# A hybrid decoder layer on one core: x's transposes become side threads, TensorE gets matmuls to run before x arrives, and the planner's account of DMA landings gets other numbers

## The chip, the core and the metric

The kernel runs on one core of a Trainium2 chip. A core has a matrix engine (TensorE, PE in the profile), a vector engine (VectorE, DVE), an activation engine (ScalarE, ACT), a general engine (GpSimd, POOL) and a sync engine (SyncE, SP), which here only issues DMAs. The engines run side by side; each works through its own list of instructions strictly in order and waits for the others on semaphores. The metric is the device time of one execution in microseconds, of which three runs are given.

## The reference, cut to what matters

One decoder layer is computed for 256 tokens of width 2048 in float32:

```
h    = rmsnorm(x, norm_mix_w)                      # x: 256 x 2048
proj = h @ w_in        # q, k, v, z, b, a, p_in, g_a, g_b  (2048 x 14368)
q,k,v = silu(causal_dwconv(q,k,v)); q,k l2-normalised per head of 128
o    = gated_delta_rule(q, k, v, g, beta)          # 16 heads, chunks of 64 in the reference
y_a  = rmsnorm(o) * silu(z)
y_b  = causal_multiscale_pool(p_in) @ pool_w * pool_scale
x   += (sigmoid(g_a) * y_a + sigmoid(g_b) * y_b) @ w_out
h    = rmsnorm(x, norm_ffn_w);  gate, up = split(h @ w_up)      # w_up: 2048 x 11264
x   += (gelu(causal_dwconv(gate) + b) * up) @ w_down            # w_down: 5632 x 2048
return rmsnorm(x, norm_final_w)
```

## The kernel before, in words

**Chunks.** Every large weight matrix is read from HBM in chunks of 256 rows by 512 columns (512 KB). `fetch` issues the DMA of a chunk into one of four `raw` buffers, `cast` rounds it on ACT to `whi`, `split` forms the rest `wlo = raw - whi` on DVE, and `gemm_a` multiplies: 12 matmuls of 128 x 512 a chunk, that is for two rows of 128 of the chunk and two blocks of 128 tokens each `xhi*whi`, `xlo*whi`, `xhi*wlo`. There are 530 chunks. In this text they are counted from 0 in the order of use: 0 to 7 are the keys of head group 0, 8 and 9 (of another shape, 8 matmuls each) feed beta and the decays, 10 to 17 are queries, 18 to 25 values; 26 to 49 are keys, queries and values of head group 1, 50 to 57 the gate z of group 0, and so on. There are four of each of `whi` and `wlo`, so the cast of a chunk cannot start before PE is done with the chunk four places earlier, and the DMA of a chunk not before the split of the chunk four places earlier.

**Order of the work.** The program is written in the order of PE's matmuls. Between them `side()` puts in other work: first the pipeline of chunks (split, cast, fetch, each when its inputs are thought to be there), then a step of one of the threads: Python generators that are started with `spawn(gen, rank)` and yield at each change of engine. A class `Plan` keeps a clock for each engine and decides when a step's turn has come. The engines execute what stands in their lists, whenever its inputs come; only the order is fixed by the plan. Its account of DMAs (`Plan.dma`, line 50) adds bytes divided by 240e3 per us to a queue, and 2 us until the landing.

**Around the change, at the start.** SP issues x in four parts of 512 columns, each followed by the DMA of a weight chunk. `x_turned(k2)` (line 411) transposes columns 256 k2 to 256 k2 + 255 of x on PE (4 transposes into a PSUM tile, `psb` for even k2, `psa` for odd), then ACT writes the rounded half `xhi` with the norm's weight as a scale (2 instructions), and DVE the rest `xlo` (2 instructions). These eight turns are called in the program's main line: turn 0 before the first GEMM, turn c + 1 from `x_next(c)`, ahead of chunk c. Threads that start there are `norms` (8 squares of x on ACT with their sums), `vectors` (small vectors, read by DMAs on ACT's queue and transposed on PE) and `matrices`.

**Around the change, later.** The work of a head group runs in threads beside the GEMMs of the next. Of it the prediction speaks of: `flip` (a DVE transpose `tn`, then 4 DMAs of 128 KB to DRAM), `decays` (`dec<-rund`, a DMA of 512 KB to all partitions, two selects on POOL, then 24 exponentials on ACT in two halves of 12, for which ACT's table may have to be loaded), and in `gdn` the solve: `cdd`, four DMAs `lb`, then 31 pairs of DVE operations `tmp` and `tb`, which get shorter from 128 x 248 on. Who holds `dec` gives it back when the last `ga` of the group before has been formed on DVE.

Of the kernel before, what the change touches and what calls it, by code (L numbers as in the profile page):

```python
# [13 lines left out]
P = 128  # L14
# [17 lines left out]
class Plan:  # L32
# [4 lines left out]
    def __init__(self):  # L37
        self.t = dict(PE=0.0, V=0.0, A=0.0, G=0.0, S=0.0)
        self.ready = self.base = 0.0
        self.queue = 0.0  # L40
        self.table = "s"

    def at(self, time):
# [6 lines left out]
    def dma(self, eng, out):  # L50
        n = 4
        for d in out.shape:
            n *= d
        self.t[eng] = max(self.t[eng], self.base) + (0.42 if eng == "S" else 0.1)
        self.queue = max(self.queue, self.t[eng]) + n / 240e3
        self.ready = max(self.ready, self.queue + 2.0)

    def op(self, eng, name, out, args, kw):
# [49 lines left out]
def kernel(  # L108
# [20 lines left out]
    plan = Plan()  # L129
# [14 lines left out]
    def nm(s):  # L144
        cnt[0] += 1
        return f"{s}_{cnt[0]}"

    def pa(shape=(P, 512)):
        return psg.tile(list(shape), F32, tag="a", name=nm("psa"))
# [7 lines left out]
    def bank():  # L157
        while len(banks) > 1 and not (banks[-2] and banks[-2] <= now["PE"]):
            yield
        banks.append(None)  # L160
        return len(banks) - 1

    def leave(n):
        banks[n] = plan.ready
# [6 lines left out]
    def take(*tags):  # L171
        while taken_by(tags):
            yield
        held.update((tag, 1e9) for tag in tags)
# [19 lines left out]
    def follow(th, step):  # L194
        if isinstance(step, tuple):
            step, th[0] = step
        th[3] = step or th[3]
        threads.sort(key=lambda th: th[:2])

    def spawn(gen, rank=1):  # L200
        cnt[0] += 1
        threads.append([rank, cnt[0], gen, None, plan.ready])
        follow(threads[-1], next(gen))
# [32 lines left out]
    def until(done):  # L236
        while not done():
            if not side():
                now["PE"] += 0.25
# [138 lines left out]
    ones = cpool.tile([P, P], F32, name="ones")  # L378
# [4 lines left out]
    epsx = cpool.tile([P, 2], F32, name="epsx")  # L383
# [11 lines left out]
    x0 = []  # L395
    for c in range(4):
# [3 lines left out]
        x0.append((xc, plan.ready))  # L400
        fetch()

    plan.at(nmready)
    nmw = cpool.tile([P, KD], F32, name="nmw")
    pv = pb()
    nc.tensor.transpose(pv[:, :KD], nmrows, ident[:KD, :KD])
    nc.vector.tensor_copy(nmw, pv[:, :KD])
    xhl = big.tile([P, KD, 2, S], F32R, tag="xhl", name="xhl")
    xhi, xlo = xhl[:, :, 0, :], xhl[:, :, 1, :]

    def x_turned(k2):
        pt = (pa if k2 % 2 else pb)([P, 2, S])
        plan.at(x0[k2 // 2][1])
        for kk in range(2):
            k = 2 * k2 + kk
            for t in range(2):
                nc.tensor.transpose(pt[:, kk, t * P : (t + 1) * P], x0[k // 4][0][:, t, (k % 4) * P : (k % 4 + 1) * P],
                                    ident)
        for kk in range(2):
            k = 2 * k2 + kk  # L420
            nc.scalar.activation(xhi[:, k, :], pt[:, kk, :], AF.Copy, scale=nmw[:, k : k + 1])
        for kk in range(2):
            k = 2 * k2 + kk
            nc.vector.scalar_tensor_tensor(xlo[:, k, :], pt[:, kk, :], nmw[:, k : k + 1], xhi[:, k, :].bitcast(F32),
                                           op0=ALU.mult, op1=ALU.subtract)

    def xh(k, t):
        return xhi[:, k, t * P : (t + 1) * P]
# [573 lines left out]
    for g in range(4):  # L1002
        vts = []
        res = []
        turns.append(res)
        done = []

        def keys(e, g=g, done=done):
            d = yield from flip(mp, e, "ev", g)
            yield from take("k", "q")  # L1010
            kq = mp.tile([P, 4, 2, S], F32, tag="kq", bufs=1, name=nm("kq"))
            done.append(kq)
            yield from conv_silu(d, 1, g, kq[:, :, 0, :])
            done.append(plan.ready)

        def queries(e, g=g, done=done):
            d = yield from flip(mp, e, "ev", g)
            while not done:
                yield
            yield from conv_silu(d, 0, g, done[0][:, :, 1, :])  # L1020
            done.append(plan.ready)

        def heads(g=g, vts=vts, res=res, done=done):
            yield "S"
            yield from take("dec0", "dec1")
            dec0 = mp.tile([P, 4, S], F32, tag="dec0", name=nm("dec0"))
            dec1 = mp.tile([P, 4, P], F32, tag="dec1", name=nm("dec1"))
            yield from decays(g, dec0, dec1)
            while len(done) < 3:
                yield  # L1030
            plan.at(max(plan.ready, *done[1:]))
            yield "PE"
            yield from take("heads")
            yield from gdn(g, done[0], vts, dec0, dec1, res)

        def values(e, g=g, vts=vts):
            d = yield from flip(mp, e, "ev", g)
            yield from take("vT")
            vT = mp.tile([P, 4, S], F32, tag="vT", bufs=1, name=nm("vT"))
            yield from conv_silu(d, 2, g, vT)  # L1040
            yield "V"
            yield from take("vt")
            vt = mp.tile([P, 2, 4, P], F32, tag="vt", name=nm("vt"))
            yield from flip_back(mp, vT, vt, "vT")
            vts.append(vt)
            vts.append(plan.ready)

        if g == 0:
            x_turned(0)

            def x_next(c):
                if c == 1:
                    plan.at(x0[0][1])
                    spawn(norms(), -1)
                if c == 2:
                    spawn(vectors(), 0)
                    spawn(matrices(), 1)
                if c < 7:
                    x_turned(c + 1)

            ps = gemm_a(xh, xl, KD, before=x_next)
            pba = pm()[:, 0, :].rearrange("p (a s) -> p a s", a=2)
            for c in range(2):
                hi, lo = weights()
                for kk in range(8):
                    k = 8 * c + kk
                    mm(pba, hi[:, kk, :], xhl[:, k], start=(k == 0), stop=(k == KD - 1))
                side()

            def start(pba=pba, heads=heads):  # L1070
                yield from strengths(pba)
                yield from heads()
        else:
            ps = gemm_a(xh, xl, KD)
        spawn(keys(evict(ps)), g)
        if g == 0:
            spawn(start(), -1)
        spawn(queries(evict(gemm_a(xh, xl, KD))), g)
        if g:
            spawn(heads(), g)  # L1080
        spawn(values(evict(gemm_a(xh, xl, KD))), g)
        if g:
            gates(g - 1)
# [215 lines left out]
```

## Time and profile before

| what | value |
|---|---|
| three runs | 1565.99, 1567.35, 1568.28 us; median 1567.35 us |
| the profiled execution | 1567.87 us, its span 1566.1 us |
| PE busy | 1540.2 us (98%), 7212 matmuls |
| DVE, ACT, POOL busy | 1036.6 us (66%), 787.2 us (50%), 68.0 us (4%) |
| HBM read / written | 309.11 MB / 23.10 MB, 212 GB/s over the span |
| granted clock of PE, mean | 0.994 |

In a row of a timeline stand the start in us from the span's start, the duration of the whole row, the engine, the source line, the operation, written tile <- read tiles, shapes and the number of instructions merged into the row; in brackets the engine's idle time ahead of it and what ended it. Nearly all rows name line 94, the wrapper that counts the plan's time. An engine's name with a q (SPq, ACTq) is the sequencer that issues DMAs. A row of waits gives the sum in us, the number of waits and the longest. A row of windows gives for a stretch the length, busy time of each engine with its number of instructions, the granted clock of PE (1.00 is full speed), the DMA engines' share and GB/s. PE's matmuls overlap, so that the spacing of their starts tells the pace and not the duration of one.

### The profile page before, as it was taken

Reading aid. Unit: us, or ns where it says so; the run is one execution under the profiler, and the core shown is the slowest. Engines: PE = TensorE matmul, PEld = TensorE weight load, DVE = VectorE, ACT = ScalarE, POOL = GpSimd, SP = SyncE. Lnnn points to the kernel's source line nnn. Section 1 sums busy time; section 2 is a strip of 40 time slices with the busy share of each in tenths; the row PEclk is TensorE's granted clock in tenths of the full one; section 3 lists DMA queues with packets and bytes.
Section 4 is the critical chain, followed back from the end, with each engine's and each line's share of the span. In section 5 each row is a group of like instructions: output and inputs, shape, how many; then the busy total and the mean of one; then the engine's idle time right before and its main releaser. Section 6 shows DMA issues by size and latency. Waiting matters only on the chain.

```text
span 1566.1 us, 19803 instructions
## 1 busy us (share of the span) xinstructions
PE 1540.2 (98%) x7212; PEld 1261.8 (81%) x7212; DVE 1036.6 (66%) x1488; ACT 787.2 (50%) x1036; POOL 68.0 (4%) x109
## 2 busy tenths in 40 slices
PE   7999999999999999999999999999999999999996
PEld 5787788787878887888888888888888888888885
DVE  4778967788778766865565666666667666544444
ACT  6474574456545854454454445454454444433334
POOL 1201000100010001000000000000000000000000
PEclk9999999999999999999999999999999999999998
DMA  7887974788568857774756888888888887665663
GB/s 227 218 257 191 264 205 140 182 253 245 147 188 234 239 162 202 191 205 133 252 179 187 246 230 233 247 248 250 243 231 232 255 244 210 233 197 191 220 195 110
DMA packets 342585, 333.52 MB, mean 213 GB/s; under 512 B 181031, under 2 KB 201559, under 8 KB 342359
## 3 DMA queue, kind: packets, MB, share of 16 engines
q1 hardware_dynamic: 339776, 327.78, 72.0%
q10 hardware_dynamic: 2710, 4.48, 0.8%
q8 instruction: 56, 0.92, 0.2%
q14 instruction: 43, 0.34, 0.1%
HBM read 309.11 MB, written 23.10 MB: 212 GB/s over the span
## 4 chain that ended last, share of the span: by engine, by line
PE 92%; DVE 3%; DMA 2%; ACT 1%; SPq 1%; issue 1%; DVEq 0%; ACTq 0%
PE psm L94 79%; PE psa L94 8%; PE psb L94 5%; DMA raw<-in_w_in_dram 2%; DVE wlo L94 1%; DVE tmp L94 1%; SPq L94 1%; DVE tb L94 1%; ACT whi L94 0%; DVE xt L94 0%; DVE tn L94 0%; DMA x<-in_x_dram 0%; ACT sqj L94 0%; DVE cy L94 0%; ACT ev L94 0%
## 5 line engine op out<-in xcount | busy, mean ns | idle before, releaser
L94 DVE TENSOR_TENSOR wlo<-raw,whi 128x1024 fp32r<-128x1024 f32 x528 | 641.4, 1222 | 409.7 <-ACT whi L94 404.2
L94 ACT CAST whi<-raw 128x1024 fp32r<-128x1024 f32 x530 | 555.7, 1052 | 621.9 <-PE psm L94 452.2
L94 PE MATMUL psm<-whi,xhl 128*128 128x512 f32 x1792 | 566.8, 398 | 4.3 <-ACT whi L94 4.0
L94 PE MATMUL psm<-whi,fhl 128*128 128x512 f32 x1408 | 433.6, 389 | 0.0
L94 PEld LDWEIGHTS psm<-whi,xhl 128*128 128x128 f32 x1792 | 334.7, 190 | 75.3 <-ACT whi L94 5.1
L94 PE MATMUL psm<-wlo,xhl 128*128 128x512 f32 x896 | 352.7, 394 | 4.2 <-DVE wlo L94 4.2
L94 PEld LDWEIGHTS psm<-whi,fhl 128*128 128x128 f32 x1408 | 264.1, 188 | 54.9
L94 PE MATMUL psm<-wlo,fhl 128*128 128x512 f32 x704 | 273.9, 389 | 0.0
L94 PEld LDWEIGHTS psm<-wlo,xhl 128*128 128x128 f32 x896 | 169.6, 189 | 43.3 <-DVE wlo L94 7.0
L94 PEld LDWEIGHTS psm<-wlo,fhl 128*128 128x128 f32 x704 | 132.1, 188 | 27.4
L94 PE MATMUL psm<-whi,hhi 128*128 128x512 f32 x176 | 68.5, 389 | 0.0
L94 PE MATMUL psm<-whi,hlo 128*128 128x512 f32 x176 | 68.5, 389 | 0.0
L94 PE MATMUL psm<-wlo,hhi 128*128 128x512 f32 x176 | 68.5, 389 | 0.0
L94 ACT ACTIVATE fev<-psm,rs 128x512 f32<-128x512 f32 x44 | 27.9, 686 | 46.2 <-PE psm L94 46.2
L94 PE MATMUL psm<-whi,mhi 128*128 128x512 f32 x128 | 50.5, 394 | 0.0
L94 PE MATMUL psm<-wlo,mhi 128*128 128x512 f32 x128 | 50.0, 390 | 0.0
L94 PE MATMUL psm<-whi,mlo 128*128 128x512 f32 x128 | 49.9, 390 | 0.0
L94 DVE SCALAR_TENSOR_TENSOR cy<-kq,cqw,cy 128x255 f32<-128x255 f32 (+2 forms) x96 | 44.1, 479 | 1.6
L94 DVE SCALAR_TENSOR_TENSOR y<-gs,cfw,y 128x255 f32<-128x255 f32 x88 | 42.6, 484 | 3.1
L94 DVE TENSOR_TENSOR tmp<-lb,tb 128x248 f32<-128x248 f32 (+30 forms) x124 | 37.1, 299 | 4.7 <-DMA lb<-cdd 1.8
L94 DVE TENSOR_TENSOR tb<-tb,tmp 128x248 f32<-128x248 f32 (+30 forms) x124 | 37.3, 301 | 4.3
L94 DVE STREAM_TRANSPOSE tn<-fev 128x1024 f32<-128x1024 f32 x22 | 27.3, 1242 | 17.1 <-ACT fev L94 15.2
(194 smaller groups left out, 1238.2 us busy)
## 6 DMA issues: line engine op xcount, KB each, us to landing
raw<-in_w_in_dram SPq DMA_DIRECT2D x226, 512.0 KB, 4.6
raw<-in_w_up_dram SPq DMA_DIRECT2D x176, 512.0 KB, 4.9
raw<-in_w_down_dram SPq DMA_DIRECT2D x88, 512.0 KB, 4.5
flip<-tn SPq DMA_DIRECT2D x136, 128.0 KB, 3.3
raw<-in_w_out_dram SPq DMA_DIRECT2D x32, 512.0 KB, 4.3
gs<-flip SPq DMA_DIRECT2D x11, 512.0 KB, 5.9
us<-flip SPq DMA_DIRECT2D x11, 512.0 KB, 6.6
kq<-flip SPq DMA_DIRECT2D x8, 512.0 KB, 6.4
```

Of the source, the lines that this page charges most:

```text
L94: r = getattr(self.eng, op)(out, *args, **kw)
```

## The change

1. `Plan`: the queue's account starts at 2.5 us instead of 0, and a DMA takes bytes / 170e3 us where the rows of its tile are at most 32 elements long, bytes / 380e3 otherwise, instead of bytes / 240e3 for all.
2. Before the DMA of the norm's weights is waited for, ACT copies a column of `epsx` to itself (which makes it load its table there), and PE runs 6 matmuls of 128 x 128 on a tile of ones; after the transpose of the norm's weights 3 more.
3. `x_turned` becomes a thread with a yield at each change of engine, and takes a PSUM bank of the plan; a turn starts once the turn four before it is done by the plan. All eight are spawned at once with rank -3 (the lowest rank goes first), and the GEMM's chunk c only waits in the plan until turn c is done.

```diff
     def __init__(self):
-        self.queue = 0.0
+        self.queue = 2.5
...
-        self.queue = max(self.queue, self.t[eng]) + n / 240e3
+        self.queue = max(self.queue, self.t[eng]) + n / (170e3 if out.shape[-1] <= 32 else 380e3)
...
+    def run_up(n):
+        warm = pa()
+        for _ in range(n):
+            tc.nc.tensor.matmul(warm[:, 0:P], ones, ones, start=True, stop=True)
+
+    tc.nc.scalar.copy(epsx[:, 0:1], epsx[:, 0:1])
+    run_up(6)
     plan.at(nmready)
...
     nc.vector.tensor_copy(nmw, pv[:, :KD])
+    run_up(3)
...
+    turned = []
 
     def x_turned(k2):
+        yield "PE"
+        while len(turned) < k2 - 3:
+            yield
+        n = yield from bank()
         pt = (pa if k2 % 2 else pb)([P, 2, S])
-        plan.at(x0[k2 // 2][1])
...
+        yield "A"
...
+        yield "V"
...
+        leave(n)
+        turned.append(plan.ready)
...
-            x_turned(0)
+            for k2 in range(8):
+                plan.at(x0[k2 // 2][1])
+                spawn(x_turned(k2), -3)
 
             def x_next(c):
+                until(lambda: len(turned) > c)
...
-                if c < 7:
-                    x_turned(c + 1)
```

No matmul of the GEMMs and no DMA is added or taken away. Since the plan's times are others, the lists of all engines are in another order in many places up to the end of the attention part. Three of these places are shown.

**ACT, from the kernel's start.** `xhl<-psb` and `xhl<-psa` are the scaled copies of a turn (even and odd k2), `CAST whi` the casts of chunks 0, 1, 2. Before:

```order
L94 ACT_TABLE_LOAD
L94 ACTIVATE xhl<-psb_122,nmw 128x256 x2
L94 ACTIVATE xhl<-psa_132,nmw 128x256 x2
L94 CAST whi_141<-raw_87 128x1024
L94 ACTIVATE xhl<-psb_160,nmw 128x256 x2
L94 CAST whi_169<-raw_91 128x1024
L94 CAST whi_179<-raw_95 128x1024
```

Now:

```order
L408 ACT_TABLE_LOAD
L408 COPY epsx<-epsx 128x1
L94 ACTIVATE xhl<-psb_135,nmw 128x256 x2
L94 CAST whi_142<-raw_87 128x1024
L94 ACTIVATE xhl<-psa_144,nmw 128x256 x2
L94 CAST whi_161<-raw_91 128x1024
L94 ACTIVATE xhl<-psb_169,nmw 128x256 x2
L94 CAST whi_183<-raw_95 128x1024
```

The casts of chunks 0 and 1 each stand one turn earlier: chunk 0's ahead of turn 1, chunk 1's ahead of turn 2.

**DVE, a little later.** `wlo` are the splits of chunks, `xhl` with `xhl` among its inputs the `xlo` of a turn. Before, from the split of chunk 3 on:

```order
L94 TENSOR_TENSOR wlo_222<-raw_99,whi_208 128x1024
L94 TENSOR_TENSOR wlo_236<-raw_151,whi_234 128x1024
L94 SCALAR_TENSOR_TENSOR xhl<-psb_244,nmw,xhl 128x256 x2
L94 TENSOR_TENSOR wlo_255<-raw_183,whi_253 128x1024
L94 SCALAR_TENSOR_TENSOR xhl<-psa_285,nmw,xhl 128x256 x2
```

Now, from the same split on:

```order
L94 TENSOR_TENSOR wlo_241<-raw_99,whi_208 128x1024
L94 TENSOR_TENSOR wlo_243<-raw_165,whi_210 128x1024
L94 TENSOR_TENSOR wlo_245<-raw_185,whi_229 128x1024
L94 TENSOR_TENSOR wlo_268<-raw_223,whi_266 128x1024
L94 SCALAR_TENSOR_TENSOR xhl<-psb_212,nmw,xhl 128x256 x2
L94 SCALAR_TENSOR_TENSOR xhl<-psa_253,nmw,xhl 128x256 x2
```

Before, the `xlo` of turn 4 stood behind the split of chunk 4; now it stands behind those of chunks 5 and 6. On PE the transposes of turns 2, 3 and 4, and 5 now stand in the middle of chunks 0, 1 and 2, those of turns 6 and 7 ahead of chunk 5; before, each stood between two chunks.

**SP, at the start of head group 1's decays.** The first row is the DMA of chunk 48, `dec` the decays of group 1, `cdd`, `lb`, `qnd` DMAs of group 0's solve. Before:

```order
L94 DMA raw_1324<-in_w_in_dram 128x2x512
L94 DMA cdd_1337<-cd_1279 128x8x32
L94 DMA kq_1342<-flip_1138 128x4x256
L94 DMA flip_1352<-tn_1333 64x16x32 x4
L94 DMA raw_1357<-in_w_in_dram 128x2x512
L94 DMA lb_1359<-cdd_1337 32x1024 x4
L94 DMA qnd_1373<-qn_1340 4x256
L94 DMA dec_226_1344<-rund 128x1024
L94 DMA raw_1384<-in_w_in_dram 128x2x512
```

Now:

```order
L94 DMA raw_1298<-in_w_in_dram 128x2x512
L94 DMA dec_232_1344<-rund 128x1024
L94 DMA flip_1369<-tn_1330 64x16x32 x4
L94 DMA raw_1374<-in_w_in_dram 128x2x512
L94 DMA cdd_1376<-cd_1321 128x8x32
L94 DMA kq_1389<-flip_1126 128x4x256
L94 DMA raw_1391<-in_w_in_dram 128x2x512
L94 DMA qnd_1393<-qn_1387 4x256
L94 DMA kq_1389<-flip_1369 128x4x256
L94 DMA raw_1440<-in_w_in_dram 128x2x512
L94 DMA lb_1442<-cdd_1376 32x1024 x4
```

The decays' DMA moved from behind `lb` and `qnd` to right behind chunk 48's. With it the rest of that stretch changed: on ACT the table load and the first 12 exponentials stood ahead of the cast of chunk 50 and now stand ahead of that of chunk 48, the second 12 stand ahead of chunk 53's in both, now with a table load before them and an eviction behind; on DVE the first 20 operations of the solve (10 pairs, with a copy ahead) stood in one piece ahead of the split of chunk 50, and now 2 stand ahead of chunk 52's and 12 with a transpose behind them ahead of chunk 53's.

## The prediction

> **What bounds the kernel now.** I read the share of busy time first (PE 98%), then PE's waits over the whole span, then the chain of waits.
>
> ```profile
> PE psm L94 <- DVE wlo L94: 4.2, 4, 3.2
> PE psb L94 <- DMA nmrows<-in_norm_mix_w_dram: 4.0, 1, 4.0
> PE psm L94 <- ACT whi L94: 4.0, 3, 1.9
> PE psb L94 <- DMA x<-in_x_dram: 1.5, 1, 1.5
> ```
>
> ```profile
> 255.45 2.68 PE psa L94 x24
> ...
> 843.03 471.96 PE psm L94 x2082
> ```
>
> PE sets the end, and no PE work is taken away: only its waits, and stretches in which it runs slower than its pace, can be won. The pace is in the chain's long piece: 471.96 / 2082 = 0.2267 us a matmul, so 12 x 0.2267 = 2.72 us a chunk; the short piece has 2.68 / 24 = 0.112 for a 128 x 128 matmul, 0.45 for the four of a turn. The waits add up to 13.7 us, and nearly all of it lies at two places, the first 20 us and about 165 us. PE's rows at the start:
>
> ```profile
> 9.61 1.22 PE L94 MATMUL psm<-whi,xhl 128*128 128x512 f32 x2 [1.86 <-ACT whi L94]
> 10.87 0.79 PE L94 MATMUL psm<-wlo,xhl 128*128 128x512 f32 x1
> ...
> 12.74 1.05 PE L94 MATMUL psm<-whi,xhl 128*128 128x512 f32 x2
> ...
> 14.76 0.60 PE L94 MATMUL psb<-ident,x 128*128 128x128 f32 x4
> 17.22 1.03 PE L94 MATMUL psm<-whi,xhl 128*128 128x512 f32 x2 [1.86 <-ACT whi L94]
> ...
> 22.35 0.71 PE L94 MATMUL psm<-whi,xhl 128*128 128x512 f32 x2
> ```
>
> Chunk 0 starts at 9.61, chunk 1 at 17.22, chunk 2 at 22.35: 7.6 and 5.1 us a step, where the pace asks 2.72 and 0.45. Two causes add up: waits for the casts, and a slow stretch (a pair of matmuls takes 1.05 at 12.74, 0.71 at 22.35). What the casts wait for shows on ACT and DVE:
>
> ```profile
> 4.59 1.28 ACT L94 ACT_TABLE_LOAD   x1 [4.59 <-DVE nmw L94]
> 6.93 0.84 ACT L94 ACTIVATE xhl<-psb,nmw 128x256 fp32r<-128x256 f32 x2 [1.06 <-PE psb L94]
> ...
> 8.52 1.04 ACT L94 CAST whi<-raw 128x1024 fp32r<-128x1024 f32 x1
> 15.39 0.84 ACT L94 ACTIVATE xhl<-psb,nmw 128x256 fp32r<-128x256 f32 x2 [5.83 <-PE psb L94]
> 16.12 1.99 ACT L94 CAST whi<-raw 128x1024 fp32r<-128x1024 f32 x2
> 18.00 0.64 ACT L94 ACTIVATE junk<-x 128x512 f32<-128x512 f32 x1
> ```
>
> ```profile
> 7.81 0.88 DVE L94 SCALAR_TENSOR_TENSOR xhl<-psb,nmw,xhl 128x256 fp32r<-128x256 f32 x2 [3.29 <-ACT xhl L94]
> ...
> 9.59 1.22 DVE L94 TENSOR_TENSOR wlo<-raw,whi 128x1024 fp32r<-128x1024 f32 x1
> ```
>
> ```profile
> 0.00:10.20 10.20, 2.81 (x10) 2.25 (x11) 2.51 (x6) 3.89 (x6) 4.67 (x21) 1.00 0.78 255
> 17.00:20.40 3.40, 2.95 (x7) 1.83 (x8) 2.50 (x3) 3.31 (x9) 0.00 (x0) 0.57 0.24 33
> 165.00:176.00 11.00, 7.85 (x22) 6.09 (x22) 10.52 (x21) 7.37 (x18) 0.00 (x0) 0.69 0.96 257
> ```
>
> ACT stood idle 5.83 us, until 15.39, for turn 2's transposes, which PE has at the end of chunk 0; the cast of chunk 1 stands behind turn 2 in ACT's list. Its data had long come: 255 GB/s x 10.20 us = 2.60 MB, five blocks of 0.524 MB, so x's first two parts and the first two chunks are in by about 10.2. The second place, at 165 us, is treated below.
>
> **The change part by part: the start.** In the new order the cast of chunk 0 stands behind one turn, not two. One turn on ACT takes 0.84, so PE's first GEMM matmul comes from 9.61 to about 8.86, and step 0 with its transposes ends at about 14.8 instead of 15.36 (14.76 + 0.60). The cast of chunk 1 now stands ahead of turn 2 and can run when its data is there, 10.2 to 11.3; its split takes 1.22 more, to 12.5. So chunk 1 starts right behind step 0, at 14.8 and not 17.22: 2.4 us ahead. With no gap there, I take it to run at pace: 2.72 + 2 x 0.45 for two turns' transposes = 3.6, to 18.4, where it was 22.35 with one turn less. PE is then 3.9 ahead, and one turn's work (0.45) further: 4.3 to 4.4; I go on with 4.3.
>
> Two waits take a part of that back. DVE now writes turn 4's `xlo` behind the splits of chunks 5 and 6. By hand from the durations above: steps 2 and 3 end at 21.7 and 24.4; ACT reaches cast 5 at 20.4, turn 5 at 21.5, cast 6 at 22.3, so split 6 runs to 24.6 and `xlo` of turn 4 to 25.5, where PE wants it behind two matmuls of chunk 4, at 24.6 (0.85 late). And six squares now stand in one piece ahead of cast 7 (0.64 each by its row, about 0.8 with the read of its sum), so that the `xlo` of turn 6 comes at about 32.2 and is wanted at 31.9. Together 1.2 to 1.3; the start gains 4.3 - 1.3 = **3.0 us**. Bounds: 4.3 if neither wait comes; near 6 if also the slow stretch of chunk 0 goes (10.87 to 14.76 is 3.89 us for 10 matmuls that take 2.27 at pace, 1.6 lost); nothing if the waits are worse by the hand chain's own error, 3 us. I stay with 3.0 since each term has its row.
>
> The run-up matmuls and the table cost nothing. What such a matmul is in the profile shows in a row by form:
>
> ```profile
> L94 PE MATMUL psa<-vt,TT 128*128 128x128 f32 x64 | 8.4, 274 | 0.0
> ```
>
> It is 32 in the code: each is 2 in the profile. So the first six are 12 x 0.112 = 1.3 us, or 2.7 if the clock is at half; they lie in PE's 4.0 us of wait for the norm's rows. The three behind it are 0.7 to 1.3 us inside the 1.5 us of wait for x. Uncovered, they would cost 2.0 to 4.0. The table load ended at 5.87, 1.06 before ACT's first use of it at 6.93: moving it wins nothing, and is 1.28 if it were in the way.
>
> **The stall at 165 us.** These rows are in the order of cause:
>
> ```profile
> 152.56 0.38 SPq L94 DMA_DIRECT2D dec<-rund  x1
> ```
>
> ```profile
> DMA to landing us min/median/max: 6.0/6.6/6.9
> ```
>
> ```profile
> 159.15 1.28 ACT L94 ACT_TABLE_LOAD   x1 [2.39 <-DMA dec<-rund]
> 160.44 2.98 ACT L94 ACTIVATE dec<-dec,shift 128x64 f32<-128x64 f32 x12
> 163.33 1.98 ACT L94 CAST whi<-raw 128x1024 fp32r<-128x1024 f32 x2
> 165.22 1.25 ACT L94 ACTIVATE ev<-psm,rs 128x512 f32<-128x512 f32 x2
> ```
>
> ```profile
> 158.26 0.42 DVE L94 TENSOR_TENSOR tmp<-lb,tb 128x248 f32<-128x248 f32 x1
> ...
> 167.03 2.35 DVE L94 TENSOR_TENSOR wlo<-raw,whi 128x1024 fp32r<-128x1024 f32 x2
> 169.30 1.24 DVE L94 STREAM_TRANSPOSE tn<-ev 128x1024 f32<-128x1024 f32 x1
> ```
>
> ```profile
> 163.72 0.39 PE L94 MATMUL psm<-wlo,xhl 128*128 128x512 f32 x1
> 164.41 0.73 PE L94 MATMUL psm<-whi,xhl 128*128 128x512 f32 x2 [0.30 <-ACT whi L94]
> 168.30 0.79 PE L94 MATMUL psm<-wlo,xhl 128*128 128x512 f32 x1 [3.15 <-DVE wlo L94]
> ...
> 174.70 0.40 PE L94 MATMUL psm<-wlo,xhl 128*128 128x512 f32 x1
> ```
>
> The DMA of the decays was issued at 152.56 and took 6.6 us; ACT sat in front of it with the cast of chunk 50 queued behind, then loaded its table and made 12 exponentials; DVE, whose order counted on a later cast, ran 20 operations of the solve, 158.26 to 167.03, ahead of the split of chunk 50. PE was held 0.46 for `whi` (the pair at 164.41 was due 0.23 behind the row ahead of it, at 163.95) and 3.4 for `wlo` (168.30 against 164.41 + 2 x 0.23 = 164.9), and then ran 15 matmuls from 168.30 to 174.70, 6.4 us for 3.4: 3.0 more, in a window with clock 0.69. Sum 0.46 + 3.4 + 3.0 = 6.9 us.
>
> In the new order the decays' DMA stands right behind that of chunk 48, about 16 us before chunk 48 is due. What it needs, 6.6 landing + 1.28 table + 2.98 exponentials + 1.05 cast + 1.2 split = 13.1, fits with 3 us to spare (the old place left 163.95 - 152.56 = 11.4). The solve is cut up. The tightest point becomes chunk 53. Its cast stands behind a table load, 12 exponentials and a pair of evictions, 1.28 + 2.98 + 1.25 = 5.5 us, and its split behind 12 operations of the solve (12 x 0.4 = 4.7) and the transpose of 1.24.
>
> ```profile
> ACT whi L94 <- PE psm L94: 15.6, 9, 3.0
> ```
>
> ACT waits here mostly for PE to free a buffer (15.6 us between 100 and 180), so a split can be ahead of its use by at most three chunks less its own work, 3 x 2.72 - 1.05 - 1.22 = 5.9 us. Against 5.5 and 5.9 us of work in front, chunk 53 comes 0 to 0.5 us late; I take 0.5: **6.9 - 0.5 = 6.4 us** won. Bounds: 6.9 if it is on time; if chunk 53 takes a wait of 3 us and the slow clock of 3 us behind it, about 1 is left, or nothing.
>
> **Elsewhere.** The old order has two short waits between 300 and 700 us, in the later head groups:
>
> ```profile
> PE psm L94 <- DVE wlo L94: 0.8, 2, 0.4
> ```
>
> Their places are reordered, and by the same account as above I find no late chunk there: 0.8 won. But four head groups have new orders everywhere, and I followed only the two places in full; for small new waits I put back 0.8, as much as the old order had. The FFN's chunks run far ahead of PE in both orders: nothing.
>
> **Sum.** 1567.87 (profiled execution) - 3.0 - 6.4 - 0.8 + 0.8 = 1558.5. The profiled execution is 0.5 above the median, 1567.35: 1558.0 us, 0.6% less.
>
> **The rivals.** *The stall moves to chunk 53.* For: the two queues in front of it are as long as what chunks can be ahead. Against: its rows fit to half a microsecond. Another microsecond late brings PE near the 3-us hold, with 3.0 of slow clock behind it; of the second place 6.9 - 6 = 1 is left: 1567.35 - 3.0 - 1 = 1563 to 1564.
>
> *The new account is too fast: slower.* The plan now takes 0.524 MB / 380e3 = 1.38 us and 2 us more, 3.4, for a chunk's DMA.
>
> ```profile
> raw<-in_w_in_dram SPq DMA_DIRECT2D x226, 512.0 KB, 4.6
> ```
>
> The profile has 4.6 for a chunk and 6.6 for the decays. Casts and work that wait on a DMA are so put into ACT's and DVE's lists earlier than their data, and what stands behind them is held, as at 159.15. Against: the old account took 2.2 + 2 = 4.2, was too fast as well, and held PE once. It decides where landings in a head group's busy stretch exceed the 3 us to spare. With such a hold of 6.9 in two of the four head groups in place of one: 1567.35 - 3.0 + 6.9 = 1571 us.
>
> *The start's gain is given back.* If the waits for `xlo` of turns 4 and 6 are worse by 3 us and chunk 53 is late too: 1567 less 0 to 2, no change that can be measured.
>
> *The run-up keeps the clock.* Chunk 0's slow stretch follows a span in which PE was mostly idle, and so did the one at 17: 0.57 in 17.00 to 20.40, behind a hold of 1.86. If the 18 trace matmuls of the run-up keep the clock up, chunk 0 saves 1.6 to 2.0 more: 1556. Against: between the run-up's end, at 5.7, and 8.86 PE has only eight transposes.
>
> The Trainium skill ("TensorE: Matmul & The Clock Gate", section "Why this matters for your kernels") asks for TensorE to be busy 4 us without a break, and says that only idle gaps over some 3 us bring the drop. By it the clock would stay up after the run-up; the trace differs in so far as a hold of 1.86 us was followed by a window at 0.57.
>
> **How the numbers follow.** The forecast has 0.45, chunk 53's stall 0.20, the slower account 0.12, the start given back 0.13, the run-up's clock 0.10. The likeliest case alone gives 1555 to 1562 (start 0 to 4.3 with the sum's others as they are, rounded inwards). Low end 1553: 1567.35 - 6 - 6.9 - 0.8, the bounds of the start and of the second place. High end 1570: the cases of no gain lie below it, and most of the slower one, under 0.12, above. A measurement of this kernel tells 0.2%, 3.1 us, from no change: faster is below 1564.2, slower above 1570.5. Faster: 0.45 + 0.10 + three quarters of 0.20 = 0.70; same: 0.05 + 0.13 = 0.18; slower 0.12.
>
> **What would show it.** PE's first `psm` row at about 8.9, chunk 1's at 14.8 with no wait for `whi`, a wait for `xhl` of DVE of about 0.8 within chunk 4; the windows from 17 on at clock 1.00. No `wlo` wait of 3 us around 160 to 170, no window of 0.69 there, and waits at chunk 53 of at most 0.5. Wrong would be: a wait of 2 us or more on `whi` or `wlo` anywhere from 100 to 800, a clock under 0.8 behind it, or ACT held by `dec` or `raw` for longer than the 2.39 of before with a cast queued behind.

## The result

The changed kernel takes 1561.23 us (median of 8 runs, 1559.39 to 1564.77), the kernel before, timed beside it, 1568.24 us (8 runs). The ratio is 0.9963, with a 95% interval from 0.9954 to 0.9972: faster by 0.37%. The forecast was 1558.0 us and 0.6%; the time lies in the range that was given. But the sum came out near the truth for other reasons than the ones written in it, as the two profiles show.

PE's waits in the changed kernel, as shown of before:

```profile
PE psm L94 <- ACT whi L94: 4.0, 2, 2.2
PE psm L94 <- DVE wlo L94: 2.8, 6, 1.2
PE psa L406 <- POOL ones L94: 1.0, 1, 1.0
PE psm L94 <- DVE xhl L94: 0.4, 1, 0.4
PE psb L94 <- DMA nmrows<-in_norm_mix_w_dram: 0.2, 1, 0.2
PE psb L94 <- DMA x<-in_x_dram: 0.2, 1, 0.2
```

The waits for the norm's rows and for x (4.0 and 1.5 before) are filled by the run-up. The waits for `wlo` fell from 4.2 to 2.8. The waits for `whi` still add up to 4.0, and the longest became longer: 2.2 instead of 1.9. Where it lies, the timeline of PE tells:

```profile
8.43 0.73 PE L94 MATMUL psm<-whi,xhl 128*128 128x512 f32 x2 [1.87 <-ACT whi L94]
...
12.56 0.73 PE L94 MATMUL psm<-whi,xhl 128*128 128x512 f32 x2
...
39.71 0.73 PE L94 MATMUL psm<-whi,xhl 128*128 128x512 f32 x2
...
167.98 0.50 PE L94 MATMUL psm<-wlo,xhl 128*128 128x512 f32 x1 [1.22 <-DVE wlo L94]
...
179.57 0.50 PE L94 MATMUL psm<-wlo,xhl 128*128 128x512 f32 x1 [0.42 <-DVE wlo L94]
...
335.30 1.05 PE L94 MATMUL psm<-whi,xhl 128*128 128x512 f32 x2 [2.16 <-ACT whi L94]
```

These are the first matmuls of chunks 0, 1 and 10, two holds in chunks 53 and 57, and the first matmul of chunk 106. These are the windows behind the two stalls in the changed kernel (the first one's row of before stands in the prediction):

```profile
165.00:176.00 11.00, 9.78 (x43) 7.80 (x42) 10.26 (x19) 3.99 (x4) 0.00 (x0) 1.00 0.98 262
335.50:339.00 3.50, 3.29 (x8) 2.07 (x8) 3.24 (x3) 3.12 (x7) 0.00 (x0) 0.51 1.01 337
```

Behind the old stall the window that had clock 0.69 now has 1.00, and PE ran 43 matmuls in it, not 22. A new slow window lies at 335.5.

**Where the time went.** The two profiled executions differ by 6.35 us (1567.87 and 1561.52). The start of the first matmul of a chunk on PE, in us, puts it in places:

| chunk | 1 | 10 | 50 | 70 | 98 | 106 | 126 | 400 |
|---|---|---|---|---|---|---|---|---|
| before | 17.2 | 45.0 | 164.4 | 226.3 | 320.9 | 342.7 | 401.2 | 1200.6 |
| changed | 12.6 | 39.7 | 158.0 | 214.6 | 310.2 | 335.3 | 393.8 | 1194.3 |
| ahead by | 4.7 | 5.3 | 6.4 | 11.7 | 10.7 | 7.4 | 7.4 | 6.3 |

The start won 5.3 us and the old stall about 5 more; then 3.3 us were given back up to the start of chunk 106, and 2 more within that chunk, in the slow window; by chunk 126, past the two short waits of the kernel before, the lead is 7.4 again. From chunk 126 to the end the two kernels differ little. (Single starts can be off by a microsecond or two, since PE's other work stands at other places between the chunks.)

### The profile page after: what moved, and what is told of

The parts are those of the page before. It is cut to its first block, busy times and chain, and to the rows that moved or that the text cites. A ratio compares the mean times of both kernels' runs of the same rounds, so it can differ in the third digit from the quotient of the medians.

```text
span 1559.8 us, 19827 instructions
## 1 busy us (share of the span) xinstructions
PE 1539.3 (99%) x7230; PEld 1261.0 (81%) x7230; DVE 1037.4 (67%) x1488; ACT 785.8 (50%) x1035; POOL 68.2 (4%) x109
## 4 chain that ended last, share of the span: by engine, by line
PE 92%; DMA 3%; DVE 2%; ACT 1%; SPq 1%; issue 0%; DVEq 0%; ACTq 0%
PE psm L94 79%; PE psa L94 7%; PE psb L94 5%; DMA raw<-in_w_in_dram 2%; SPq L94 1%; ACT whi L94 1%; DVE wlo L94 1%; DMA lb<-cdd 0%; DMA kq<-flip 0%; DVE xt L94 0%; DMA cdd<-cd 0%; DVE tmp L94 0%; DVE tb L94 0%; DVE cy L94 0%; ACT sqj L94 0%
## 5 line engine op out<-in xcount | busy, mean ns | idle before, releaser
L94 PEld LDWEIGHTS psm<-whi,hlo 128*128 128x128 f32 x176 | 33.1, 188 | 6.9
```

The costliest lines, as they stand in the source:

```text
L94: r = getattr(self.eng, op)(out, *args, **kw)
```

## The experiments

In all of them "chunk n" is the start of its first matmul on PE. The times are medians; each ratio is against the kernel before on the same chip. Since the median of the kernel before moved from 1566.74 to 1568.24 us between the sets of runs, kernels from different sets are better compared by their ratios.

### Run-up away, and run-up alone

From the changed kernel, nothing else moved:

```diff
-    tc.nc.scalar.copy(epsx[:, 0:1], epsx[:, 0:1])
-    run_up(6)
...
-    run_up(3)
```

> The changed kernel without its nine run-up matmuls and without the early copy on ACT; the order of all other instructions is the changed kernel's on every engine. In the changed kernel chunk 10 starts on PE at 39.71 us and PE is at full clock from 4.45 us on; in the kernel before it is at 45.01, and the clock is at half up to 14.06 and again from 17.48 to 20.89. Theory A, the run-up lifted the clock ahead of chunk 0: without it chunk 0 runs at half clock for 3 to 5 us, chunk 10 starts 1.5 to 3 us later (41.2 to 42.7), total 1562.7 to 1564. Rival B, the order of the turns alone gave the gain, the clock follows the missing holds: chunk 10 within 0.3 us of 39.71, total 1561.2.

Measured: 1561.49 us, ratio 0.9974 (0.9964 to 0.9983). At the start theory A held: chunk 0 ran at half clock (the clock became full at 15.06 us) and chunk 10 came at 41.52 instead of 39.71.

```profile
8.44 1.22 PE L94 MATMUL psm<-whi,xhl 128*128 128x512 f32 x2 [1.02 <-ACT whi L94]
...
10.29 1.05 PE L94 MATMUL psm<-whi,xhl 128*128 128x512 f32 x2
...
336.59 0.73 PE L94 MATMUL psm<-whi,xhl 128*128 128x512 f32 x2 [1.92 <-ACT whi L94]
```

In chunk 0's first pair of matmuls one sees the clock: 1.22 us here, 0.73 in the changed kernel. In the two profiles nothing of the 1.8 us was left later on. Chunk 98 was still 2.5 us behind the changed kernel's, chunk 126 only 0.2 (394.0 and 393.8). What lies between is the new stall: a PE that comes later waits less there (1.92 us for `whi`), and without a slow window behind it. The totals do not settle it: by the medians 0.3 us are left (less than A had), by the ratios 0.11%, or 1.7 us, and the intervals overlap.

The other way round, the kernel before with the run-up and the early copy:

```diff
+    tc.nc.scalar.copy(epsx[:, 0:1], epsx[:, 0:1])
+    run_up(6)
     plan.at(nmready)
...
+    run_up(3)
```

> The kernel before plus the nine run-up matmuls and the early copy on ACT; the order of everything else as before. Theory A: chunk 0 runs at full clock, ends 1.5 to 2 us earlier, and with it turn 2's transposes and the cast of chunk 1; the hold of 1.86 us ahead of chunk 1 stays. Chunk 10 at 41.5 to 43.5 instead of 45.01, total 1564.7 to 1566.7. Rival B (the run-up does nothing for the clock behind a gap of 1.9 us): chunk 10 at 45.0, total 1568.2.

Measured: 1566.23 us, ratio 0.9994 (0.9985 to 1.0003). Chunk 10 came at 42.90, as A said, so the run-up was worth 2.1 us at the start in these two profiles, but not by A's way alone: the clock fell to half from 9.21 to 12.63 us, so chunk 0 was not at full clock throughout, and the slow stretch from 17.48 to 20.89 did not come. With no new stall behind it the gain was kept in the profile (chunk 126 at 398.8 instead of 401.2). The median of the total moved by 0.6, which cannot be told from no change.

### Each half of the change alone

The new numbers of the queue account alone, in the kernel before:

```diff
-        self.queue = 0.0
+        self.queue = 2.5
...
-... + n / 240e3
+... + n / (170e3 if out.shape[-1] <= 32 else 380e3)
```

> The kernel before with the new numbers of the queue account alone; x's turns and the start as before, and behind the first 40 us the order of all engines is that of the changed kernel. Theory A: the account wins most of the stall at 165 us (6.9 to about 2) and loses about as much at a new one at 332 us (2.2 us of wait for whi with a slow clock of 3.4 us behind it, 4.5 in all): 1567.2, within 0.2% of before. Rival B, the stall at 332 us comes from the earlier start and its shift of the timing against the DMAs: no hold over 1 us there, total 1562 to 1563.

Measured: 1570.27 us, ratio 1.0018 (1.0009 to 1.0028): not faster, if anything a little slower. Theory A was right about both stalls. Here are PE's waits between 300 and 400 us in this kernel, and one row from its start:

```profile
PE psm L94 <- ACT whi L94: 1.7, 1, 1.7
PE psm L94 <- DVE wlo L94: 1.1, 2, 0.5
```

```profile
22.61 0.80 PE L94 MATMUL psm<-wlo,xhl 128*128 128x512 f32 x1 [3.49 <-DVE wlo L94]
```

The total was missed by 3 us, and the second row shows why. With the old way of calling the turns, the new numbers put casts and splits of the first chunks into an order in which PE waits 3.49 us for a `wlo` of chunk 2. Behind that hold the clock was at half from 21.26 to 28.09 us, and chunk 10 came at 48.2, 3.2 later than before.

The changed kernel with the old numbers:

```diff
-        self.queue = 2.5
+        self.queue = 0.0
...
-... + n / (170e3 if out.shape[-1] <= 32 else 380e3)
+... + n / 240e3
```

> The changed kernel with the old numbers of the queue account; threads, run-up and table load stay. Theory A: the start wins 4 to 5.3 us at chunk 10, the stall at 165 us stays with 5 to 7 us, no stall at 332 us: 1562.9 to 1564.2. Rival B, the shift of the start by itself takes the decays' DMA out of the way of chunk 50: stall under 2 us, total 1557 to 1559.

Measured: 1564.65 us, ratio 0.9986 (0.9977 to 0.9995). The total is just above A's range, and one clause of A fell: there is a stall around 340 us here as well (a wait of 2.7 us for `wlo` in chunk 108), though the account is the old one. The first stall stayed, at chunk 57 instead of 50, with a wait of 2.8 us for `whi`. So the halves do not add up: 0.18% slower and 0.14% faster alone, 0.37% faster together. The threads repair the start that the new numbers spoil, and the new numbers thin out the first stall, which the threads alone only shift.

### What makes the new stall

What stands ahead of chunk 106 in the changed kernel shows on SP and ACT:

```profile
304.68 1.98 SPq L94 DMA_DIRECT2D lb<-cdd  x4
306.76 7.85 SPq L94 DMA_DIRECT2D back<-tb  x4
314.71 0.60 SPq L94 DMA_DIRECT2D raw<-in_w_in_dram  x1
...
319.14 0.92 SPq L94 DMA_DIRECT2D dec<-rund  x1
320.74 7.70 SPq L94 DMA_DIRECT2D flip<-tn  x4
328.54 2.60 SPq L94 DMA_DIRECT2D raw<-in_w_in_dram  x4
```

```profile
327.92 1.28 ACT L94 ACT_TABLE_LOAD   x1 [1.43 <-DMA dec<-rund]
329.22 2.98 ACT L94 ACTIVATE dec<-dec,shift 128x64 f32<-128x64 f32 x12
334.21 1.04 ACT L94 CAST whi<-raw 128x1024 fp32r<-128x1024 f32 x1 [2.01 <-DMA raw<-in_w_in_dram]
```

The single `raw` row at 314.71 is chunk 102's, the first of the four at 328.54 is chunk 106's. Chunk 102's DMA could have gone out when its buffer came free, with the split of chunk 98, which ended at 304.40; it went out ten microseconds later. SP was busy issuing: the four `back` took 7.85 us, where they took 3.67 in the kernel before, and the four `flip` 7.70. And `back` is the piece that moved. In the kernel before these four were issued at 272.74, long ahead of that group's `lb`:

```profile
272.74 3.67 SPq L94 DMA_DIRECT2D back<-tb  x4
...
311.33 2.07 SPq L94 DMA_DIRECT2D lb<-cdd  x4
```

`back` transposes the values of head group 1, after their convolution, and the group's convolutions go one behind the other through one buffer (`cy`). In the kernel before, the first four operations on its keys ran on DVE ahead of group 0's solve:

```profile
152.61 0.96 DVE L94 SCALAR_TENSOR_TENSOR cy<-kq,cqw,cy 128x255 f32<-128x255 f32 x2
...
154.62 0.87 DVE L94 SCALAR_TENSOR_TENSOR cy<-kq,cqw,cy 128x253 f32<-128x253 f32 x2
```

In the changed kernel none ran before 200.76:

```profile
200.76 1.91 DVE L94 SCALAR_TENSOR_TENSOR cy<-kq,cqw,cy 128x255 f32<-128x255 f32 x4
```

From there the whole row of convolutions is later, and its end falls into the next head group's busy stretch. In both halves tried alone `back` also stands behind `lb` (314.03 and 316.03 us, 310.69 and 317.69), and both have the stall; in the kernel before, and in it with the run-up, it stands 13 chunks earlier, and the waits for `wlo` between 300 and 400 us are 0.8 and 1.7 us, with none for `whi`.

To test it, the last convolution and `back` of group 1 were given a higher rank in the changed kernel:

```diff
-                    yield "V"
+                    yield ("V", -1) if kind == 2 and g == 1 else "V"
...
             yield from flip_back(mp, vT, vt, "vT")
+            yield "S", g
```

> The changed kernel with one thing moved: the last convolution of head group 1's values and the transposition behind it (the four DMAs `back`) get a higher rank, so that `back` is issued behind chunk 94's DMA, where it stood behind chunk 101's and behind the four `lb` (in the kernel before it stood behind chunk 88's). Theory A, the new stall of 4.5 us around 333 us comes from `back` standing beside `lb` and ahead of chunk 102's DMA: no hold over 1 us between 300 and 360 us, PE reaches chunk 126 at 389 to 390.5 (393.8 in the changed kernel), total 1556.5 to 1558.5. Rival B, the DMA engines are simply full there and a PE that comes earlier must wait: a stall of 3 us or more stays, total 1560 to 1561.5.

Measured: 1557.50 us, ratio 0.9937 (0.9923 to 0.9950). PE has no wait at all between 300 and 400 us, and chunk 126 came at 386.4, earlier than A said. (1.2 us of its lead over the changed kernel, 7.4, were there at chunk 60, ahead of everything that was moved: in this execution chunk 53 waited 0.55 us instead of 1.22.) SP in this kernel:

```profile
313.27 1.73 SPq L94 DMA_DIRECT2D lb<-cdd  x4
315.10 0.93 SPq L94 DMA_DIRECT2D pnt<-qnd  x2
316.07 0.51 SPq L94 DMA_DIRECT2D raw<-in_w_in_dram  x1
316.62 0.47 SPq L94 DMA_DIRECT2D dec<-rund  x1
318.10 5.54 SPq L94 DMA_DIRECT2D flip<-tn  x4
```

Chunk 106's DMA, the `raw` row, went out at 316.07, 12 us earlier, and ahead of the decays and the flips. (The profiled execution was the fastest of the six, 1554.56; the gain over the changed kernel is 3.7 us by the medians, 4.1 by the ratios.) Rival B, full DMA engines whatever the order, fell.

The same place was then tested with smaller moves. With `back` held until the DMAs of chunks 102 and 103 are issued:

```diff
+        while turn == 1 and len(raws) < 104:
+            yield
         d = dpool.tile([S, 512], F32, tag="back", name=nm("back"))
```

> The changed kernel, `back` of head group 1 held until the DMAs of chunks 102 and 103 are issued; by it chunk 106's DMA also comes ahead of the decays' and the four `flip`. Nothing else of weight moves. Theory A (the place of `back` in SP's list): chunk 102's DMA is issued at about 307 instead of 314.7, chunk 106's by 323 instead of 328.5; the hold ahead of chunk 106 is under 1 us; chunk 126 at 389.5 to 391; total 1557 to 1559. Rival B (DMA engines full): stall of 3 us or more stays, 1560 to 1561.5.

Measured: 1562.18 us, ratio 0.9971 (0.9959 to 0.9982): no gain. Chunk 102 and 106 were on time, as A said (issued at 307.90 and 318.28), but A did not look one chunk further:

```profile
320.67 8.57 SPq L94 DMA_DIRECT2D flip<-tn  x4
329.34 1.91 SPq L94 DMA_DIRECT2D raw<-in_w_in_dram  x3
```

```profile
336.82 0.73 PE L94 MATMUL psm<-whi,xhl 128*128 128x512 f32 x2 [2.40 <-ACT whi L94]
```

Now it is chunk 107 whose DMA stands behind the four flips, and PE waits 2.40 us for it, with a slow window behind (339.06 to 342.48). With the flips held instead, behind the DMAs of chunks 106 and 107:

```diff
+        while turn == 7 and len(raws) < 107:
+            yield
         d = dpool.tile([512, S], F32, tag="flip", bufs=4, name=nm("flip"))
```

> The changed kernel, only the four `flip` that stand ahead of chunk 106's DMA are held until the DMAs of chunks 106 and 107 are issued. Chunk 106's DMA then goes out at about 322 instead of 328.5. Theory A: its cast stays behind the table load and 12 exponentials of the decays, which ended at 332.2, so the cast ends at 333.3 and the hold falls from 2.2 us to 0.3 to 0.5, its split about 1 us late, no slow clock: 2 to 3.5 us won, total 1557.8 to 1559.3. Rival B (DMA engines full, or the decays' DMA is what holds): hold of 2 us or more stays, total 1560 to 1561.5.

Measured: 1560.65 us, ratio 0.9957 (0.9944 to 0.9971). The hold fell to one wait of 1.21 us for `wlo`, with no slow window, which is A's mechanism, a chunk later than A had it (in chunk 107). The total is within the interval of the changed kernel's. In this profiled execution the start was 1.1 us worse, which hides a part (see the last section). So, by these rows, the stall is not one misplaced DMA: `back`, `lb`, `dec` and `flip` together are more than the four buffers bridge, and of the three moves tried only taking `back` out of that stretch cured it.

The cure also tells about the run-up and the account. The kernel with `back` early, without run-up and early copy:

```diff
-    tc.nc.scalar.copy(epsx[:, 0:1], epsx[:, 0:1])
-    run_up(6)
...
-    run_up(3)
```

> The kernel with `back` issued early (1557.5 us) without the run-up matmuls and the early copy; everything else in the same order. In the changed kernel the run-up brought chunk 10 1.8 us forward (39.71 against 41.52 without), and nothing of it was left at the end (1561.2 against 1561.5). Theory A, the stall at 333 us took it back, since PE waited there for a DMA: with that stall gone the run-up is worth its 1 to 1.8 us, total 1558.5 to 1559.3 without it. Rival B, the run-up does not last in most executions, as the clock falls again behind the hold ahead of chunk 0: total within 0.5 of 1557.5.

Measured: 1558.82 us, ratio 0.9947 (0.9934 to 0.9961), against 0.9937 (0.9923 to 0.9950) with them. The medians differ by 1.3 us in the direction of A; the intervals overlap, so this agrees with A and does not prove it. By the ratios the run-up is worth 0.10% here and 0.11% with the stall, so the totals do not show that the stall took its gain; that rests on the profiles (chunks 98 and 126 above). In the profile chunk 10 was only 0.3 us later (40.1 and 39.8), since the clock rose early in this execution, at 11.9 us.

The account alone with the same move:

```diff
-        self.queue = 0.0
+        self.queue = 2.5
...
-        self.queue = max(self.queue, self.t[eng]) + n / 240e3
+        self.queue = max(self.queue, self.t[eng]) + n / (170e3 if out.shape[-1] <= 32 else 380e3)
...
-                    yield "V"
+                    yield ("V", -1) if kind == 2 and g == 1 else "V"
...
             yield from flip_back(mp, vT, vt, "vT")
+            yield "S", g
```

> The kernel before with the new numbers of the queue account alone (1570.3 us as such) and head group 1's `back` issued early by a higher rank. Theory A: its stall of 5.2 us at 340 us goes, the stall at 165 us stays small, and the start stays as in the kernel with the account alone (chunk 10 at 45 to 48.2): total 1563 to 1565. Rival B, without the earlier start the place of `back` is not what holds chunk 106: total 1569 to 1570.5.

Measured: 1564.30 us, ratio 0.9985 (0.9976 to 0.9995), inside A's range: the stall is gone here too (no wait of PE from 300 to 400 us), 6 us less than the account alone by the medians, 5 by the ratios. Not all of this need be the stall: in its profile, the fastest of ten executions, the hold at 22.61 us is there too (3.47 us), but cost no clock, and chunk 10 came at 45.7, 2.5 us ahead of the account alone.

### The old stall, one chunk relieved

In the kernel before, chunk 50's cast put ahead of the table load, and its split into the solve:

```diff
         for j in range(B0 - 1):
             yield "V"
+            if g == 0 and j == 4:
+                ready = plan.ready
+                for done, step in ((raws, fetch), (rounded, cast), (made, split)):
+                    while len(done) <= 50:
+                        step()
+                plan.at(ready)
```

> The kernel before with chunk 50's cast put ahead of the table load and the exponentials of the decays, and its split behind 8 of the 20 operations of the solve. The decays' DMA stays where it was. Theory A (the stall at 165 us is the order on ACT and DVE behind a late DMA): the hold of 3.2 us and the slow clock behind it go, at most 1.5 us stays at chunks 50 to 53; PE reaches chunk 60 at 192 to 193.5 (198.1 before), total 1561 to 1562.5 if that is kept to the end. Rival B, what is won there is taken back later, as PE then meets the next late DMA around 350 us: chunk 60 as under A, total 1564 to 1566.

Measured: 1569.16 us, ratio 1.0007 (0.9998 to 1.0016): nothing won. Both theories were wrong about the place itself:

```profile
167.30 0.50 PE L94 MATMUL psm<-wlo,xhl 128*128 128x512 f32 x1 [1.57 <-DVE wlo L94]
...
172.95 0.50 PE L94 MATMUL psm<-wlo,xhl 128*128 128x512 f32 x1 [2.61 <-DVE wlo L94]
```

Chunk 50 was on time, and PE waited 1.57 us for chunk 51's split and 2.61 for chunk 52's, 4.2 us in all, with a slow stretch behind it again (173.71 to 177.13). The exponentials and the solve were still in front of somebody. What the new account did is another thing: it moved the first half of the exponentials out to 144 us and cut the solve into pieces.

### A version with more run-up

The early `back` kernel with six more run-up matmuls between turn 1's transposes and chunk 0:

```diff
             def x_next(c):
                 until(lambda: len(turned) > c)
+                if c == 0:
+                    run_up(6)
```

> The kernel with `back` issued early, and six more run-up matmuls between turn 1's transposes and chunk 0, where PE waits 1.9 us for the first cast. By the clock records so far full clock was granted for 3.41 us or a multiple, and taken away behind some of the starts with the same hold (at 10.27 us in the run with the flips held, at 10.93 with the old account, at 9.21 in the kernel before with run-up), not behind others (from 4.45 and 4.88 on to the end of the stretch). Theory A, it depends on how the holds fall into these stretches, and a PE that is busy in them keeps the clock: full clock throughout, chunk 10 at 39.5 to 40, total 1556.5 to 1557.5. Rival B, the matmuls stand in the way of chunk 0 and delay it by up to 1.3 us: chunk 10 at 40.5 to 41, total 1558 to 1559.

Measured: 1556.13 us, ratio 0.9934 (0.9922 to 0.9947), the fastest of all, though not told apart from the early `back` kernel by the intervals. The clock was not full throughout: in the profile it rose at 10.25 us, in the very moment when chunk 0 began, and stayed. Chunk 0 itself began 1.8 us later than in the early `back` kernel (10.32 and 8.53), since PE was still busy with the run-up at half clock, as rival B had it; PE then had no wait and no slow clock up to chunk 10, which came at 40.07, between A's range and B's. So the profile does not show A's mechanism, and what makes this kernel's median the lowest stays open.

## Why the prediction was right and wrong

**What bounds the kernel** held: PE was 98% busy, and all that was won and lost was waits and slow clock.

**The start** was forecast at 3.0 us and gave 5.3 (chunk 10). The direction of each row was right: chunk 0 came at 8.43 (8.9 forecast), chunk 1 followed without a wait for `whi`, at 12.56 (14.8 forecast), and the new wait for `xlo` within chunk 4 came, with 0.4 us (0.85 forecast). The failed step is "The run-up matmuls and the table cost nothing": the sum has them at 0, and full clock from the run-up was a rival with a chance of 0.10, at 1.6 to 2.0 us. In the profile the clock was full from 4.45 us on, and the transposes of turns 0 and 1 and chunk 0 ran at pace, but for a wait of 0.53 us for chunk 0's `wlo`. The run without run-up puts 1.8 of the 5.3 us on it and 3.5 on the turns, close to the 3.0; in the pair of profiles with `back` early the run-up was worth only 0.3. The second wait that was charged, for `xlo` of turn 6, came too, but is too short for the list of waits:

```profile
23.03 0.50 PE L94 MATMUL psm<-whi,xhl 128*128 128x512 f32 x1 [0.38 <-DVE xhl L94]
...
29.32 1.03 PE L94 MATMUL psm<-whi,xhl 128*128 128x512 f32 x2
...
30.42 0.63 PE L94 MATMUL psm<-whi,xhl 128*128 128x512 f32 x2
```

The second row is chunk 6's first pair, whose second matmul began when DVE had written that `xlo`, about 0.3 us late (0.3 forecast).

**The clock rule.** The rule of the Trainium skill that the prediction quotes ("TensorE: Matmul & The Clock Gate", section "Why this matters for your kernels") would have kept the clock up behind the run-up, and the trace agrees in the profiled execution of the changed kernel, behind a hold of 1.87 us. It does not agree in the execution with the flips held, where the same start with holds of 1.33 and 0.53 us lost it at 10.27 us.

**The stall at 165 us** was forecast to shrink from 6.9 to 0.5, at chunk 53. It shrank to about 2: chunk 53's `wlo` was 1.4 us late (a wait of 1.22 and the 0.2 of a restart), chunk 57's 0.6 (a wait of 0.42). The mechanism was right, chunk 53 was the place, and the clock stayed full. The term that was mis-sized is "chunk 53 comes 0 to 0.5 us late":

```profile
158.41 1.05 ACT L94 CAST whi<-raw 128x1024 fp32r<-128x1024 f32 x1 [1.11 <-DMA raw<-in_w_in_dram]
```

```profile
159.49 1.23 DVE L94 TENSOR_TENSOR wlo<-raw,whi 128x1024 fp32r<-128x1024 f32 x1 [1.44 <-ACT whi L94]
...
165.58 1.24 DVE L94 STREAM_TRANSPOSE tn<-ev 128x1024 f32<-128x1024 f32 x1
166.74 4.59 DVE L94 TENSOR_TENSOR wlo<-raw,whi 128x1024 fp32r<-128x1024 f32 x4
```

The first two rows are the cast and the split of chunk 52, the last is chunk 53's split with the three behind it. From the end of chunk 52's split, 160.72, to the start of the next, DVE had 6.0 us of work (5.9 forecast), and chunk 53, whose first matmul came at 166.14, got its `wlo` 1.4 late. But chunk 52's split was not 5.9 us ahead of its use: it ended 2.7 us ahead of PE's 163.42, since its cast had waited 1.11 us for its DMA, and the cast of chunk 51 before it 2.46 us. The prediction took the most that a split can be ahead for what it is. Rival one, the stall that moves to chunk 53, came true in part: 1.4 us and no slow clock where it was priced at 6.

**Elsewhere** was forecast at 0, and that step failed outright: "by the same account as above I find no late chunk there". The two waits of 0.8 us went, and one of 2.16 with a slow stretch came, 4.5 us in all. This is what the prediction itself had named as a sign of being wrong: "a wait of 2 us or more on `whi` or `wlo` anywhere from 100 to 800, a clock under 0.8 behind it". The hand check looked at how far splits stood ahead of their use. It did not look at the DMAs that had left their place 13 chunks earlier, nor at how long SP takes to issue four of them there (7.85 us). The rival on the slower side had named a hold in another head group, at 6.9 us in two of them; it came in one, at 4.5. Its reason was another: not casts that stand ahead of their data because the account is too fast, since the old account with the new start has a stall at the same place, but background work that fell behind and met the next group's.

**The sum**: -5.3 - 4.9 + 4.5 - 0.8 = -6.5 by the measured terms, against -6.35 between the two executions and -9.4 forecast. The start was too small by 2.3, the old stall too large by 1.5, and 4.5 were not seen. That the time fell into the range, and even into the likeliest case's own (1555 to 1562), owes something to these errors' opposite signs, and is in so far luck.

## What to carry to other kernels

When an order changes everywhere, compare not only the places with stalls: list where each background DMA stood before and stands now, and look at every one that moved by several weight chunks, above all those that now meet another group's DMAs on the same issuing queue. A gain ahead of such a place need not be kept until the place itself is cured: in the profiles here 1.8 us won at the start were gone 300 us later. The stall that had two queues of work in front of it was not cured by relieving one chunk; the work had to leave the stretch.

## What the runs showed of the hardware

**The clock moves in steps of 3.41 us.** The trace's record of granted clock gives the times of its changes. The start of four executions (us, granted share from then on):

```
before                       14.06 full,  17.48 half,  20.89 full
changed                       4.45 full
flips held (same start)       6.86 full,  10.27 half,  13.68 full
changed, old account          4.10 full,  10.93 half,  14.34 full
```

The stretches between two changes are here one or two times 3.41 us long, but they begin at another point in each execution. (Up to the first change the column of the windows reads 1.00, while matmuls 0.43 us apart show half.) The length of a hold alone does not tell whether it costs the clock. The clearest pair is the account alone and the account with `back` early, whose chunk 2 starts at 18.42 and 18.43 us and is then held for 3.49 and 3.47 us, to 22.61 in both. In the first the borders of the stretches lie at 17.85 and 21.26, and the clock was at half from 21.26 to 28.09; in the second they lie 0.3 us earlier, at 17.55 and 20.96, and it stayed full. Ahead of chunk 0 the changed kernel held 1.87 us, across a border, and kept it. In the run with the flips held, the stretch from 6.86 to 10.27 contained holds of 1.33 and 0.53 us, and the next was slow:

```profile
6.80:10.20 3.40, 1.54 (x7) 0.87 (x7) 2.10 (x3) 2.67 (x6) 0.00 (x0) 1.00 1.05 404
10.20:13.60 3.40, 3.40 (x11) 2.71 (x11) 2.13 (x4) 1.88 (x4) 0.00 (x0) 0.51 1.05 386
```

PE was busy 1.54 of 3.40 us in the first of these windows and got a clock of 0.51 in the second. A limit of busy time that decides did not come out of the runs: in the changed kernel with the old account PE was busy 1.49 of the 3.41 us from 178.18 to 181.59, and the clock stayed full. The stretches are as the Trainium skill has them ("TensorE: Matmul & The Clock Gate", section "Part 1: The HAM clock gate (the "warmup" mystery)"): a window of about 3.4 us that does not start with the kernel. The trace agrees on the length (3.41) and on the free start. What the run-up was worth at chunk 10 differed with it: 1.8, 2.1 and 0.3 us in the three pairs of profiles with and without it.

**Issuing a DMA of short rows can hold the issuing queue for microseconds.** One `flip` or `back` of 128 KB took SP about 0.67 us to issue in the median (0.58 the shortest `back`), but single ones took up to 4.84 us, while in the same kernel a weight chunk of 512 KB from `w_in` took 0.37 in the median and 1.06 at most:

```profile
L94 SPq DMA_DIRECT2D back<-tb x16: 582/667/4844, 155.1 to 619.2; - x16
```

(shortest, median and longest in ns, of the changed kernel). Everything behind it in SP's list waits, the weights too. Two windows of the changed kernel, in which some of these four `back` and four `flip` were being issued:

```profile
310.00:315.00 5.00, 5.00 (x24) 4.14 (x23) 2.99 (x5) 2.91 (x5) 0.00 (x0) 1.00 0.69 115
320.00:325.00 5.00, 4.74 (x20) 3.28 (x18) 3.01 (x3) 2.53 (x3) 0.00 (x0) 1.00 0.99 344
```

The DMA engines were full in the second (share 0.99) but not in the first (0.69, and 115 GB/s), so that engines that are full on the mean do not explain it alone: while the last of the four `back` was being issued, 1.79 us from 312.83 on, the share was 0.57. What limits the issue was not tried and stays open.
